# The pool of the small statistics tiles placed below the weights' buffers instead of above them

## The chip, the cores and the metric

The kernel runs on one core of a Trainium2 chip. The metric is the device time of one execution in microseconds (us); the time of a kernel is the median of its runs.

## The reference, cut to what matters

Two transformer blocks are applied one after the other to one sequence of 1024 tokens with 1024 features, all in float32. In outline:

```python
# block 1 (modulated by c; a context of 256 tokens takes part in its mixer)
x = x + g1 * token_mixer(modulate(rmsnorm(x), sh1, sc1), h_ctx)   # gated linear attention, spatial mix
x = x + g2 * swiglu(modulate(rmsnorm(x), sh2, sc2), w_ffn_in, w_ffn_out)
x = rmsnorm(x)
# block 2
proj = rmsnorm(x) @ w_in
x = x + (gate_a * rg_lru(...) + gate_b * banded_attention(...)) @ w_out
x = x + (silu(ff_gate) * ff_up) @ w_ffn_out                       # ff_gate, ff_up from rmsnorm(x) @ w_ffn_in
x = rmsnorm(x)
```

Nearly all of the work is in products of the activations (1024 tokens) with weights of 1024 by 1024 up to 1024 by 5632.

## The kernel before, in words

Activations lie feature-major, as tiles of 128 features by 512 tokens (float32, 2048 bytes per partition), one for each half q of the tokens. To reach float32's accuracy with float32r products, each operand is held as an exact sum of two parts, hi and lo, and each k step of a product is three matmuls: weight hi by activation hi, weight hi by activation lo, weight lo by activation hi. `gemm` (L163 to L165) does this for blocks of 128 by 128 weights, held stationary, and 512 tokens that move. `gemm_tok` (L175 to L177) turns the roles round: 128 tokens of the activations are stationary and 256 columns of weights move. `ffn_in` (L1051 to L1053) and `ffn_out` (L1264 to L1266) have their own three lines, with products by the scheme of Strassen and Winograd.

A block of weights goes through `unit` (L139 to L152): a DMA on SP's queue brings it into a tile of the pool raw, ScalarE copies it as the hi part into a tile wh (L150), and GpSimd, or VectorE, subtracts to get the lo part, a tile wl (L151). In the FFN the weights come into tiles of 512 columns, and `split` (L192, L193) writes half a wh and half a wl.

Order: the program is written out by hand. `proj` gives the products of one block of weights, `step` does them one after the other and after each of them `tick` takes one step of what runs beside them (norms, decays, the heads' attention), and in block 2 also half way through a product. Waits between engines are set by the framework from the tiles' uses.

Storage: SBUF pools are opened in `__init__` (L59 to L69) and lie one after the other in the order of their opening. Sizes are per partition.

- cst: constants, among them vt, ident and ones.
- raw: 2 tiles of 4096 bytes. wp: 4 tiles wh and 4 tiles wl of 4096 bytes. tmp: 4 tiles t512 of 2048 bytes.
- sm: the statistics tiles, 4 each of ms, rsy, rst, es and ast (32 bytes), 4 of et (64 bytes), and lc0 to lc4 once (64 bytes).
- hp: 32 tiles hl of 2048 bytes, for split activations.
- After hp come the pools of a phase: ada (2 tiles of 512 bytes), slots or lru (tiles of 4096 bytes), halves (44 tiles half of 2048 bytes), in block 2's mixers also kq, vhl, p, pt, bias and ot, all of sizes that are multiples of 512 bytes.

`ffn_out`, L1206 to L1215, does the last of its blocks of hidden features (4 k steps) in another way: all eight units of weights are loaded ahead and kept, and their parts lie in tiles hl of the pool hp, not in wh and wl:

```python
kept.append(self.unit(wo[m][:, cols], kt=n, into=[self.part(), self.part()]))
```

Its moving operands are tiles half. These products are at the end of each block's FFN, with 512 tokens in block 1 and for the first half of the tokens in block 2, and with 256 for the second half there.

Of the kernel before, what the change touches and what calls it, by code (L numbers as in the profile page):

```python
# [16 lines left out]
P = 128  # L17
T = 1024
# [31 lines left out]
def hs(q):  # L50
    """The columns of half q of the tokens."""
    return slice(q * HQ, q * HQ + HQ)


class Prog:
    """Activations lie feature-major, [features on partitions, tokens], in tiles of 128
    features by 512 tokens; operands of the large products as exact sums of two float32r parts."""

    def __init__(self, tc, ins, out, ctx):  # L59
        self.tc, self.nc, self.I, self.out = tc, tc.nc, ins, out  # L60
        self.cst = self.pool(ctx, "cst", 1)
        self.raw = self.pool(ctx, "raw", 2)
        self.wp = self.pool(ctx, "wp", 4)
        self.tmp = self.pool(ctx, "tmp", 4)
        self.sm = self.pool(ctx, "sm", 4)
        self.hp = self.pool(ctx, "hp", 32)
        self.dr = self.pool(ctx, "dr", 1, space=bass.MemoryType.DRAM)
        self.bg, self.lag, self.loads = deque(), deque(), 0

# [28 lines left out]
    def slot(self, *dims, dt=F32):  # L98
        """[P, 1024] of the phase's storage, or less of it in the shape dims."""
        return self.shaped(self.sp.tile([P, T], dt, name="slot"), dims)  # L100
# [7 lines left out]
    def half(self, dt=F32):  # L108
        """[P, 512] of the phase's storage."""
        return self.gp.tile([P, HQ], dt, name="half")  # L110
# [4 lines left out]
    def hnew(self, n=8):  # L115
        """A split activation, hi and lo, each n tiles of features by halves of tokens."""
# [22 lines left out]
    def unit(self, src, kt=8, width=P, eng=None, raw=None, into=None):  # L139
        """Load one block of weights (if it isn't in raw yet) and split it exactly into two float32r parts."""  # L140
# [13 lines left out]
    def wide(self, src, eng=None, raws=(None, None)):  # L154
        """Two blocks, 1024 x 256 together."""
        return [self.unit(src[i], kt=4, width=256, eng=eng if i else None, raw=raws[i]) for i in range(2)]

    def gemm(self, o, w, h, l, q, kt=8, s=slice(None), mid=None):
        """o[feature, token] = W^T X with both operands split; mid comes half way."""
# [9 lines left out]
    def gemm_tok(self, o, ws, h, l, t):  # L169
        """o[token, feature] = X W for the 128 tokens of block t."""  # L170
# [8 lines left out]
    def proj(self, src, fn, mid=None):  # L179
        """The products of one block of weights with both halves of the tokens."""  # L180
# [15 lines left out]
    def tick(self, n=1):  # L196
        """The next step of what runs beside the large products."""
# [14 lines left out]
    def store(self, dst, src):  # L212
        """A store that later loads need not wait behind."""
        self.lag.append((self.loads + 2, dst, src))
# [6 lines left out]
    def step(self, chunks, n=1):  # L221
        """One product after the other, with n steps of what runs beside them after each."""
# [5 lines left out]
    def square_into(self, acc, src, first, scale=1.0, eng=None):  # L228
        """acc += (scale * src)^2"""
# [6 lines left out]
    def squares(self, acc, src, eng):  # L236
        """The sum of the squares of tiles."""
# [4 lines left out]
    def token_sums(self, accs, ps, o):  # L242
        """ps[:, o + b] = sums over features for the tokens of block b."""
# [6 lines left out]
    def rsqrt(self, x):  # L250
        """1/sqrt of a small positive tile, by Newton's steps from the exponent's half."""
# [12 lines left out]
    def spread(self, r):  # L264
        """r holds a value for each token, tokens on partitions in blocks: the same on all
        partitions, tokens along the free axis."""
# [6 lines left out]
    def rstd(self, accs, n=D):  # L273
        """1/sqrt(mean of the squares + eps) in a bank, from sums of squares, in two steps."""
# [10 lines left out]
    def now(self, steps):  # L285
        """All steps at once."""
# [6 lines left out]
    def modulated(self, x, rs, A, B, hi, lo, eng=None):  # L293
        """hi + lo = x * A * rs + B"""
# [10 lines left out]
    def norm(self, q, acc, A, B=None):  # L305
        """Steps to the modulated norm of half q of self.x, in the form that ffn_in takes: with quarters Bij
        (i: half of the features, j: of the tokens), B11, B21, B22 and the sums T1..T4, all split."""
# [54 lines left out]
    def ada_first(self):  # L362
        """Shift and scale of the first norm, for the latents and the context, one half of the features after
        the other, by products; most of the scale by sums of weighted rows over k first. In steps."""
# [45 lines left out]
    def ada_one(self, m):  # L410
        """A block of gate 1, shift 2, scale 2, gate 2 of the latents; its sums over k and those of the
        block before over the partitions."""
# [19 lines left out]
    def ada_last(self):  # L432
# [5 lines left out]
        # the branches are summed twice as large  # L438
# [3 lines left out]
    def start(self):  # L442
# [5 lines left out]
        # resets of the scans at the chunks' first tokens  # L448
# [56 lines left out]
    def start_latents(self):  # L505
        """Steps to the norm of the latents."""
# [15 lines left out]
    def decays(self, st, n, zs, d):  # L522
        """Cumulated log decays (times GATE_TEMP) of direction d within each chunk, in steps.
        st: stacked low-rank inputs [96, n]; gives tiles that hold [P, NH, n] in order."""
# [29 lines left out]
    def low_rank(self, waf, st, h, l, n, q):  # L554
        """Inputs of the decays, stacked [hi; lo; hi]."""
# [23 lines left out]
    def latent_decays(self, stl, zs):  # L579
        """Decays of the latents, kept outside."""  # L580
# [36 lines left out]
    def context_states(self, st, zs):  # L617
        """Steps to the states that the context leaves, for both directions."""
        nc = self.nc
        self.Si = self.slots_of(2, NH, 256)  # L620
        for d in QS:
# [7 lines left out]
            # the half that is passed first decays through the other one too  # L629
# [17 lines left out]
    def ends(self, c, d):  # L647
        """Of chunked log decays: the chunks' totals, their exponentials, those of pairs."""
# [10 lines left out]
    def transposed(self, x):  # L659
        """Each block of 128 columns of x, transposed."""  # L660
# [9 lines left out]
    def gla_consts(self):  # L670
# [3 lines left out]
        for d in QS:  # L674
# [3 lines left out]
            # partition = key j, column = query i; forward j <= i  # L678
# [4 lines left out]
        # half of the norm's gain, for twice the silu  # L683
# [3 lines left out]
    def gla_proj(self, h, B):  # L687
        """Queries, keys and values of a head."""
# [20 lines left out]
    def gla_decayed(self, h, d, B):  # L709
        """Keys and queries with the decays of direction d."""  # L710
# [17 lines left out]
    def gla_dir(self, h, d, B, X):  # L728
        """Steps of one direction of a head."""
# [4 lines left out]
        for g in QS:  # L734
            ps = self.ax_bank()
            for i in range(4):
# [3 lines left out]
                # keys of the half passed first against queries of the other  # L740
# [51 lines left out]
    def gla_head(self, h, B):  # L792
        """Steps of a head: both directions, then the norm of the sum."""
# [27 lines left out]
    def gla_out(self, h, B, parts=None):  # L821
        """The gated output of a head, kept outside or split."""
# [17 lines left out]
    def gate_unit(self, nm, m, dst):  # L840
        """tanh of half a branch gate: its sigmoid is half of 1 + that."""
# [46 lines left out]
    def load_heads(self, parts):  # L888
        """Steps to the output of all heads, split; the last one's comes in its own way."""
# [21 lines left out]
    def spatial(self):  # L911
# [25 lines left out]
        # spatial weights, and the part of the mix that the shift of the norm and the bias give  # L937
# [55 lines left out]
    def residual(self, src, wo, h, l, scale, norm):  # L993
        """self.x = src + scale * (h + l) @ wo, one half of the tokens after the other, and the
        norm of each half"""
# [19 lines left out]
    def ffn_in(self, wi, hid):  # L1015
        """hid = silu(W_gate^T h) * (W_value^T h), by the products of Strassen's scheme in Winograd's form:
        the quarters of W^T are Aij (i: gate or value, j: half of the features)."""
# [55 lines left out]
        def ahead(f):  # L1073
            """The parts of A and their sums in the order of the products."""
# [23 lines left out]
        # the first products do without the second half of the tokens  # L1098
# [27 lines left out]
    def ffn_out(self, wo, hid, xs, scale, pieces, squares, norm, extra=lambda: iter(())):  # L1126
        """x += scale * FFN(h), by blocks of hidden features: plain products, or those of Strassen's scheme in
        Winograd's form (with quarters by pairs of tiles of x, halves of the block and halves of the tokens). The
        last block's sums come in pieces (half, columns), each followed by what norm gives for it."""
# [7 lines left out]
        def plain(f0, n, H):  # L1137
            """Steps to the operands of plain products."""
# [10 lines left out]
        def forms(f0, n, X):  # L1149
            """Steps to the operands of the scheme's products."""  # L1150
# [44 lines left out]
        def room(w):  # L1195
            """The next half of a buffer of weights, its two parts."""
# [5 lines left out]
        def supply():  # L1202
            """The weights of all products in order, each with its share of the buffers."""
# [73 lines left out]
        def residue():  # L1277
            """Steps that add what x was."""
# [92 lines left out]
    def between(self, q, accs, gg):  # L1371
        """Steps of the final norm of the first block, then the first norm of the second, for half q."""
# [9 lines left out]
        # 1 / sqrt(m1) / sqrt(m2 / m1 + eps) = 1 / sqrt(m2 + eps * m1)  # L1382
# [23 lines left out]
    def lru_consts(self):  # L1406
        """c8 = -8 softplus(-lambda) / 2, and halves of the gate biases."""
# [5 lines left out]
        # log1p(e) = 2 atanh(e / (2 + e))  # L1413
# [16 lines left out]
    def lru_front(self, j, F):  # L1430
        """The convolved input, also split."""
# [20 lines left out]
    def lru_gates(self, j, F):  # L1452
        """Products of the gates of both directions."""
# [16 lines left out]
    def lru_rest(self, j, F):  # L1470
        """Pieces of the gated linear recurrences; twice their values are halved here."""
# [12 lines left out]
        def rate(d):  # L1484
            # 1 - a^2 = tanh(-log a) (1 + a^2)
# [20 lines left out]
    def attention_consts(self):  # L1506
        """Distance and window terms of all heads, kept outside, in steps."""
# [6 lines left out]
        # 0 inside the window, -1e30 outside  # L1514
# [8 lines left out]
    def keys_values(self):  # L1523
        """Keys and values of all heads, kept outside."""
# [26 lines left out]
    def att_group(self, G):  # L1551
        """Keys of a group as [hi; hi] and [lo; lo], values as [hi | lo]."""
# [314 lines left out]
```

## Time and profile before

| | |
|---|---|
| median of 3 runs | 3458.62 us |
| lowest and highest run | 3456.98 and 3459.93 us |
| span of the profiled execution | 3453.9 us |
| TensorE busy | 3305.8 us, 15,868 matmuls |
| TensorE weight loads busy | 2683.4 us |
| VectorE, ScalarE, GpSimd busy | 2118.4, 1364.3, 1544.3 us |
| granted TensorE clock, mean | 0.985 |

The profile is of one execution; its span goes from the first to the last instruction, and the page gives no other time of that execution. The runs shown lie 3.1 to 6.0 us above the span, their median 4.7 us. PE is TensorE's matmul, PEld its weight load, DVE VectorE, ACT ScalarE, POOL GpSimd, SP the queue that issues most DMAs. Matmuls are pipelined: one of 512 columns is shown as some 0.4 us long while the next starts after 0.23 us, so that the pace is read from starts or from counts, not from durations. Times of windows count from the span's start. In a line such as `mm<-half,wh` the output stands first, then the moving operand, then the stationary one.

### The profile page before, as it was taken

The numbers are of one execution on the slowest core, as the hardware profiler recorded it, in microseconds if no ns is written. First come the engines' busy times: TensorE is split into PE (matmuls) and PEld (weight loads), VectorE is DVE, ScalarE is ACT, GpSimd is POOL, SyncE is SP. The second block draws the span as 40 slices with busy tenths as digits, with TensorE's granted clock in tenths as the row PEclk, the third lists the DMA queues.
The fourth block names the chain that finished last, engine by engine and source line by source line (L and its number), as shares of the span: only waits on it lengthen the run. The fifth ranks groups of instructions, "written<-read, shape, count | busy, mean of one in ns | idle before, by whom it ended". The sixth has DMA issues, their size and how long they took to land. (4 is left out here: it accounts for less than half of the span.)

```text
span 3453.9 us, 43238 instructions
## 1 busy us (share of the span) xinstructions
PE 3305.8 (96%) x15868; PEld 2683.4 (78%) x15868; DVE 2118.4 (61%) x3438; ACT 1364.3 (39%) x2396; POOL 1544.3 (45%) x991
## 2 busy tenths in 40 slices
PE   7999999999999999999999989999999999999997
PEld 4778888888888778888767867777777778887766
DVE  7554234333667385555698587777776585554786
ACT  4552222211122442232424486666665332232433
POOL 3222233222322675444656434444444775444764
PEclk9999999999999999999999999999999999999999
DMA  6121111244236522221352311111114432222342
GB/s 254 62 110 53 49 68 65 74 159 129 84 119 204 169 92 80 74 82 67 113 177 83 130 33 54 45 54 45 54 48 154 144 103 99 74 80 89 95 137 78
DMA packets 153012, 335.11 MB, mean 97 GB/s; under 512 B 20864, under 2 KB 29184, under 8 KB 152800
## 3 DMA queue, kind: packets, MB, share of 16 engines
q1 hardware_dynamic: 140640, 311.36, 26.8%
q10 hardware_dynamic: 12160, 20.98, 1.6%
q8 instruction: 126, 2.06, 0.2%
q14 instruction: 86, 0.70, 0.1%
HBM read 263.07 MB, written 69.21 MB: 96 GB/s over the span
## 5 line engine op out<-in xcount | busy, mean ns | idle before, releaser
L151 POOL TENSOR_TENSOR wl<-raw,wh 128x1024 fp32r<-128x1024 f32 (+1 forms) x188 | 426.7, 2273 | 751.2 <-ACT wh L150 629.9
L163 PE MATMUL mm<-hl,wh 128*128 128x512 f32 (+1 forms) x1584 | 643.3, 406 | 1.4 <-ACT t L1547 1.4
L165 PE MATMUL mm<-hl,wl 128*128 128x512 f32 (+1 forms) x1584 | 630.7, 398 | 1.6 <-POOL wl L151 1.6
L164 PE MATMUL mm<-hl,wh 128*128 128x512 f32 (+1 forms) x1584 | 631.7, 399 | 0.0
L193 POOL TENSOR_TENSOR wl<-half,wh 128x512 fp32r<-128x512 f32 x308 | 433.0, 1430 | 367.5 <-ACT wh L192 367.5
L150 ACT CAST wh<-raw 128x1024 fp32r<-128x1024 f32 (+3 forms) x189 | 177.4, 940 | 492.3 <-PE mm L164 232.4
L165 PEld LDWEIGHTS mm<-hl,wl 128*128 128x128 f32 (+1 forms) x1584 | 300.5, 190 | 74.6 <-POOL wl L151 2.4
L163 PEld LDWEIGHTS mm<-hl,wh 128*128 128x128 f32 (+1 forms) x1584 | 300.2, 190 | 66.6 <-ACT t L1547 1.8
L164 PEld LDWEIGHTS mm<-hl,wh 128*128 128x128 f32 (+1 forms) x1584 | 300.5, 190 | 64.9 <-issue 0.5
L192 ACT CAST wh<-half 128x512 fp32r<-128x512 f32 x308 | 178.6, 619 | 409.6 <-PE ax L1052 218.1
L1030 DVE TENSOR_TENSOR half<-half 128x512 f32<-128x512 f32 x176 | 202.1, 1188 | 3.0
L1606 POOL TENSOR_SCALAR p<-p,ast 128x384 f32<-128x384 f32 (+1 forms) x64 | 84.0, 1313 | 263.4 <-DVE ast L1604 162.5
L175 PE MATMUL mm<-wh,hl 128*128 128x256 f32 x576 | 163.5, 284 | 1.3 <-ACT wh L150 1.3
L177 PE MATMUL mm<-wl,hl 128*128 128x256 f32 x576 | 161.8, 281 | 1.9 <-POOL wl L151 1.9
L176 PE MATMUL mm<-wh,hl 128*128 128x256 f32 x576 | 162.2, 282 | 0.7 <-DVE hl L193 0.5
L1052 PE MATMUL mm<-hl,wh 128*128 128x512 f32 x360 | 142.8, 397 | 3.3 <-POOL hl L193 3.3
L1051 PE MATMUL mm<-hl,wh 128*128 128x512 f32 x360 | 142.6, 396 | 0.6 <-ACT hl L192 0.6
L1053 PE MATMUL mm<-hl,wl 128*128 128x512 f32 x360 | 142.4, 395 | 0.0
L1051 PE MATMUL ax<-hl,wh 128*128 128x512 f32 x344 | 136.5, 397 | 0.8 <-ACT hl L192 0.7
L1053 PE MATMUL ax<-hl,wl 128*128 128x512 f32 x344 | 136.2, 396 | 0.0
L1052 PE MATMUL ax<-hl,wh 128*128 128x512 f32 x344 | 136.0, 395 | 0.0
L193 POOL TENSOR_TENSOR wl<-raw,wh 128x384 fp32r<-128x384 f32 x96 | 113.8, 1204 | 37.1 <-ACT wh L192 37.1
(419 smaller groups left out, 7991.7 us busy)
## 6 DMA issues: line engine op xcount, KB each, us to landing
half<-in_w_fi SPq DMA_DIRECT2D x196, 256.0 KB, 4.7
hid<-t SPq DMA_DIRECT2D x78, 256.0 KB, 2.0
half<-hid SPq DMA_DIRECT2D x72, 256.0 KB, 4.5
raw<-in_w_ada SPq DMA_DIRECT2D x32, 512.0 KB, 3.7
raw<-in_w_o SPq DMA_DIRECT2D x32, 512.0 KB, 3.9
raw<-in_w_fo SPq DMA_DIRECT2D x32, 384.0 KB, 3.2
slot<-in_w_ada SPq DMA_DIRECT2D x16, 512.0 KB, 10.2
raw<-in_w_u SPq DMA_DIRECT2D x16, 512.0 KB, 3.6
```

Source lines behind the costliest of these rows:

```text
L150: nc.scalar.copy(hi, r)
L151: self.last_split = (eng or nc.gpsimd).tensor_tensor(lo, r, hi.bitcast(F32), op=ALU.subtract).ins
L163: mm(o, wh[:, k], h[k][q][:, s], start=k == 0, stop=False)
L164: mm(o, wh[:, k], l[k][q][:, s], start=False, stop=False)
L165: mm(o, wl[:, k], h[k][q][:, s], start=False, stop=k == kt - 1)
L175: mm(o, h[k][q][:, s], wh[:, k % 4], start=k == 0, stop=False)
L192: self.nc.scalar.copy(hi, x)
L193: (eng or self.nc.vector).tensor_tensor(lo, x, hi.bitcast(F32), op=ALU.subtract)
L1030: V.tensor_tensor(s, a, b, op=op)
L1051: mm(o, wh[:, k], h, start=k == 0, stop=False)
L1052: mm(o, wh[:, k], l, start=False, stop=False)
L1053: mm(o, wl[:, k], h, start=False, stop=k == 3)
```

## The change

In `__init__` the pool sm is opened right after cst, ahead of raw, wp and tmp, instead of after tmp. Nothing else in the code differs; comments and docstrings are gone.

```diff
         self.cst = self.pool(ctx, "cst", 1)
+        self.sm = self.pool(ctx, "sm", 4)
         self.raw = self.pool(ctx, "raw", 2)
         self.wp = self.pool(ctx, "wp", 4)
         self.tmp = self.pool(ctx, "tmp", 4)
-        self.sm = self.pool(ctx, "sm", 4)
         self.hp = self.pool(ctx, "hp", 32)
         self.dr = self.pool(ctx, "dr", 1, space=bass.MemoryType.DRAM)
```

## Rows read from the trace of the kernel before

**Rows 1.** The page's first part: busy us (share of the span) xinstructions.
```profile
PE 3305.8 (96%) x15868; PEld 2683.4 (78%) x15868; DVE 2118.4 (61%) x3438; ACT 1364.3 (39%) x2396; POOL 1544.3 (45%) x991
```

**Rows 2.** Windows: stretch, us, PE, PEld, DVE, ACT, POOL busy (x), PEclk, DMA share, GB/s.
```profile
110.00:660.00 550.00, 538.86 (x3022) 458.18 (x3021) 213.37 (x300) 175.16 (x251) 141.88 (x59) 0.98 0.19 67
660.00:820.00 160.00, 156.82 (x703) 126.65 (x702) 64.43 (x131) 30.67 (x44) 42.97 (x22) 1.00 0.45 147
...
920.00:1200.00 280.00, 278.26 (x1275) 226.94 (x1276) 173.06 (x295) 79.25 (x114) 108.70 (x58) 0.99 0.47 158
1200.00:1650.00 450.00, 443.10 (x1890) 353.01 (x1890) 275.90 (x331) 144.65 (x253) 243.33 (x171) 1.00 0.23 80
1650.00:1860.00 210.00, 193.79 (x790) 150.40 (x789) 179.87 (x227) 79.90 (x156) 132.03 (x100) 0.97 0.40 132
1860.00:2660.00 800.00, 753.31 (x3659) 613.09 (x3658) 587.96 (x1172) 514.75 (x964) 340.50 (x192) 0.98 0.19 64
2660.00:3170.00 510.00, 504.10 (x2158) 402.08 (x2157) 297.87 (x363) 161.79 (x276) 290.39 (x197) 1.00 0.29 100
3170.00:3390.00 220.00, 206.24 (x845) 157.44 (x844) 155.35 (x197) 80.60 (x161) 145.47 (x115) 0.98 0.38 120
```

**Rows 3.** Windows, same columns: inside ffn_in, inside the kept block of block 1.
```profile
1300.00:1600.00 300.00, 300.00 (x1287) 241.74 (x1286) 169.75 (x200) 86.70 (x153) 148.59 (x108) 1.00 0.23 81
1862.00:1886.00 24.00, 24.00 (x107) 19.87 (x106) 15.35 (x23) 14.90 (x24) 7.08 (x5) 1.00 0.25 78
```

**Rows 4.** Timeline of PE in ffn_in: start us, us, engine, line, op, tiles.
```profile
1399.83 0.39 PE L1052 MATMUL ax<-half,wh 128*128 128x512 f32 x1
1400.06 0.40 PE L1053 MATMUL ax<-half,wl 128*128 128x512 f32 x1
...
1402.40 0.40 PE L1051 MATMUL mm<-half,wh 128*128 128x512 f32 x1
```

**Rows 5.** Timeline of PE at the start of the kept block, same columns.
```profile
1859.00 0.39 PE L163 MATMUL mm<-half,hl 128*128 128x512 f32 x1
...
1860.39 0.39 PE L163 MATMUL mm<-half,hl 128*128 128x512 f32 x1
...
1862.88 0.39 PE L165 MATMUL ax<-half,hl 128*128 128x512 f32 x1
```

**Rows 6.** Windows, matmuls that read wl alone: stretch, us, PE busy (x), PEclk, DMA.
```profile
110.00:660.00 550.00, 242.24 (x688) 0.98 0.19 67
660.00:820.00 160.00, 86.53 (x222) 1.00 0.45 147
...
920.00:1200.00 280.00, 145.56 (x367) 0.99 0.47 158
1200.00:1650.00 450.00, 247.08 (x626) 1.00 0.23 80
1650.00:1860.00 210.00, 106.27 (x262) 0.97 0.40 132
1860.00:2660.00 800.00, 320.13 (x820) 0.98 0.19 64
2660.00:3170.00 510.00, 280.84 (x711) 1.00 0.29 100
3170.00:3390.00 220.00, 111.09 (x278) 0.98 0.38 120
```

**Rows 7.** Windows, columns of rows 2: inside gemm_tok of the spatial mix.
```profile
845.00:875.00 30.00, 30.00 (x257) 30.00 (x257) 10.29 (x45) 6.34 (x13) 4.84 (x3) 1.00 0.30 106
```

**Rows 8.** Timeline of PE, kept block of block 2 with 256 columns.
```profile
3413.04 0.28 PE L165 MATMUL ax<-half,hl 128*128 128x256 f32 x1
...
3415.20 0.28 PE L165 MATMUL mm<-half,hl 128*128 128x256 f32 x1
```

**Rows 9.** The page's DMA issues: tiles, queue, count, KB each, us to landing.
```profile
half<-in_w_fi SPq DMA_DIRECT2D x196, 256.0 KB, 4.7
...
raw<-in_w_o SPq DMA_DIRECT2D x32, 512.0 KB, 3.9
```

## The prediction

> **What bounds the kernel now.** I read the page's busy times first, then stretches of the run one by one, then the starts of single products. TensorE is busy 3305.8 of the 3453.9 us [rows 1], but matmuls overlap, so this alone does not say at what pace they run. By stretches [rows 2], the PE column covers 98 to 100% of 660 to 1650 us and of 2660 to 3170 us at a granted clock of 0.99 to 1.00, while VectorE stays under 62% and GpSimd under 58% there. In these stretches only a shorter distance from one matmul to the next can shorten the run. In 1650 to 1860 and 3170 to 3390 PE has 92 and 94%, and 1860 to 2660 has 94% with VectorE at 73%: there PE also waits, and a faster PE gives part of its gain back as a longer wait. 110 to 660 has 98%, but its products are cut up by the small ones of the attention heads.
>
> So the distance of the products is the question. From 1300 to 1600 us PE does nothing but 512-column products of ffn_in, whose weights lie in wh and wl: 1286 weight loads in 300 us are 233.3 ns each [rows 3]. From 1862 to 1886 us it does nothing but products of the same shape (128 rows by 128 columns by 512, L163 to L165, four k steps) whose weights lie in hl, since ffn_out's last block keeps its weights in the activations' pool: 106 loads in 24 us, 226.4 ns each. The starts say the same: 11 steps in 2.57 us are 233.6 ns [rows 4], 11 steps in 2.49 us are 226.4 ns [rows 5]. Clock (1.00), moving operand (half) and reading engine are the same; VectorE, ScalarE and GpSimd work beside both. What differs is where the weights lie.
>
> **What the change moves.** sm holds per partition four each of ms, rsy, rst, es and ast (32 bytes) and et (64 bytes), and lc0 to lc4 once (64 bytes): 4 x 224 + 320 = 1216 bytes, which is 2 x 512 + 192. Raw (2 x 4096), wp (8 x 4096) and tmp (4 x 2048) are 49,152 bytes, 96 x 512. Before, hp follows sm, so hl and all pools above it (whose tiles are multiples of 512 bytes) lie 192 bytes off wh and wl modulo 512. After, sm sits below, raw, wp and tmp move up by 1216, and hp stays where it was: weights and activations have one phase, as hl and half have now in the block at 1862 us. The sm tiles move down by 96 x 512 and keep their phase. The phases agree even modulo 2048, as in that block, since 49,152 is 24 x 2048. No instruction, wait or DMA is added, removed or reordered on any queue, SP's and POOL's included.
>
> **The price of one product.** I take the two settled steps as the prices: 233.3 - 226.6 = 6.7 ns saved by each 512-column product with weights in wh or wl. 226.4 is not there at once: after the switch to the kept weights the first six steps take 1.39 us, 231.7 ns each, and only then comes 226.4 [rows 5]. A run that is broken every dozen products by other work would thus spend half of it unsettled, and I count nothing for these steps.
>
> Here a rule of the Trainium skill speaks against the change. Its page "TensorE: Matmul & The Clock Gate", section "Step-by-step: what each phase is for", says that PE has two independent read ports into SBUF, so that loading the next weights takes nothing from the running matmul. By it the place of the weights is without effect and the sum would be 0; the two settled steps, 233.3 and 226.4, leave a difference which it does not account for.
>
> **The sum.** Each k step has two products with wh and one with wl, so the products are three times the count of wl [rows 6], less the 640 k steps of gemm_tok where wl is the moving operand: by the code 256 in 110 to 660 (values of four heads), some ten at the end of 660 to 820 and 64 in 1860 to 2660, the rest outside the table. For each stretch: products, the share that runs settled (from the length of unbroken runs in the code: whole units of 24 and more, against attention with 12 or less), and the share of the gain that stays on the path.
> - 1200 to 1650 (ffn_in): 1878 x 0.95 x 1.0 = 1784, 12.0 us.
> - 2660 to 3170 (w_out and ffn_in of block 2): 2133 x 0.95 x 0.95 = 1925, 12.9 us.
> - 920 to 1200: 1101 x 0.80 x 0.9 = 793, 5.3 us. 660 to 820: 639 x 0.85 x 0.9 = 489, 3.3 us.
> - 110 to 660 (heads of block 1): 1296 x 0.65 x 0.4 = 337, 2.3 us.
> - 1860 to 2660 (mixers): 2268 x 0.35 x 0.6 = 476, 3.2 us. The scores, softmax and turned weights of a block wait for each other on VectorE and ScalarE, so much of the time between two waits of PE is theirs.
> - 1650 to 1860 and 3170 to 3390 (ffn_out): 1620 x 0.75 x 0.3 = 365, 2.4 us. The next limit there is the split weights and VectorE's sums, which do not get faster.
> Together 41.4 us. The path shares of 1 and 0.9 are read from PE's coverage; 0.3 to 0.6 are choices between 0 and 1, and the range carries both ends.
>
> Against it, gemm_tok: its 256-column products have hl as weights and wh, wl as the moving operand, and they too come into one phase. They now take 30 us for 257 [rows 7], 117 ns; the kept block's 256-column products, already of one phase, take 18 steps in 2.16 us, 120.0 ns [rows 8]. 1920 x 3 ns are up to 5.8 us of loss; the two rows differ in operand roles, so the other end is 0. I take 4.4 us.
>
> Other engines: the splits, loads and sums on raw, wh, wl and t512 now start 192 bytes further on. Transfers into half already start there and take 4.7 us, those into raw 3.9 us [rows 9]; the sizes differ, so this bounds a dearer landing at 0.8 us. It is covered by the two raw buffers and up to four of wh and wl that are filled ahead of PE. I cost it at nothing; without that cover (the first unit of a stage) some ten loads would cost 8 us. A gain for these engines is as possible and also hidden.
>
> Sum: 41.4 - 4.4 = 37.0 us, about 1.1%. The span of 3453.9 would become 3416.9. The median of the runs shown, 3458.62, lies 4.7 above that span; the same distance gives 3421.6, and I say 3421.6.
>
> **The rivals.**
> (a) No effect, 3459 to 3463: the kept weights are faster for another reason (they were written long before, or lie far from address 0), and 0 to 4.4 us of gemm_tok remain. For: by the code only 288 products have 512 columns and kept weights. Against: VectorE, ScalarE and GpSimd are at work in both windows of [rows 3], so it is not their traffic that makes the difference. Also here: the pools are not placed in the order in which they are opened, so that no phase changes.
> (b) Slower, 3486: one phase is what costs. The 256-column rows show it, 120 against 117 ns; if products on freshly written weights in wp behave like those, 10,965 x 3 ns x 0.65 on the path + 5.8 = 27 us. Place: every product with wh or wl. It decides once the mean step rises by 0.2 ns (7 us is the bound of no change, less gemm_tok's 5). Against: the same shape with 512 columns is shorter at one phase.
> (c) Only long streams gain, 3438: runs cut by other work never settle or return all to their waits, and 12.0 + 12.9 - 4.4 = 20.5 us are left. For: the six slow steps after each break. Nearly the same time, 3441, comes out if nothing settles and every product saves 1.6 ns as these six do.
>
> **How the numbers follow.** Forecast 0.73, (c) 0.13, (a) 0.09, (b) 0.05. The range reaches from all path shares at 1 and no loss in gemm_tok, 8090 x 6.7 = 54.2 us, 3404, to (c), 3440; (a) and (b) stay outside. 0.2%, some 7 us, is about what a measurement of this kernel can tell from no change: faster 0.86, same 0.09, slower 0.05.
>
> **What would show it.** Right: 300 us inside ffn_in hold 1323 loads instead of 1286, the steps there are 0.23 and 0.22 us in turn, gemm_tok's go to 0.12; PE's coverage in 1200 to 1650 and 2660 to 3170 stays, these stretches shorten by about 12 us each, and PE's waits grow in ffn_out. Wrong: settled steps of 233 ns in ffn_in with kept ones still at 226 (a), or above 234 (b); or 226 in ffn_in but no shortening behind it, so that a wait I do not see took it.

## The result and the profile after

The changed kernel takes 3423.12 us (median of 4 runs, 3417.93 to 3424.86) against 3457.95 for the kernel before (median of 4), a ratio of 0.9897, 95% interval 0.9883 to 0.9911. The prediction said 3421.6 and 3404 to 3440. The profiled execution's span goes from 3453.9 to 3422.2 us.

The page's first part after the change, against [rows 1]: as many matmuls, 45.7 us less of PE, 11.9 more of its weight loads, the other engines within 9 us of what they had.

```profile
PE 3260.1 (95%) x15868; PEld 2695.3 (79%) x15868; DVE 2126.6 (62%) x3438; ACT 1363.1 (40%) x2396; POOL 1539.2 (45%) x991
```

The pace, against [rows 3]: windows (stretch, us, PE, PEld, DVE, ACT, POOL busy with counts, PEclk, DMA share, GB/s) inside ffn_in and inside the kept block of block 1.

```profile
1290.00:1590.00 300.00, 300.00 (x1325) 248.51 (x1324) 178.59 (x209) 88.23 (x157) 151.84 (x111) 1.00 0.24 80
1839.00:1863.00 24.00, 24.00 (x107) 19.88 (x106) 17.81 (x25) 13.08 (x22) 5.90 (x6) 1.00 0.29 88
```

In ffn_in 300 us now hold 1324 weight loads, 226.6 ns each, where 1286 stood; the prediction asked for 1323. The kept block, whose weights did not move against its activations, has 106 as before. One load lasts as long as it did, 187.7 ns against 188.0 (PEld's time by its count); it is the distance from product to product that shrank. The timeline of PE in ffn_in, against [rows 4], shows the new step:

```profile
1389.71 0.39 PE L1051 MATMUL ax<-half,wh 128*128 128x512 f32 x1
...
1392.20 0.39 PE L1053 MATMUL ax<-half,wl 128*128 128x512 f32 x1
```

Eleven steps in 2.49 us, 226.4 ns, which is the kept block's settled step [rows 5].

Where the 31.7 us of span came from is read by cutting the new run at the same matmuls at which the old one was cut in [rows 2] (each border is the new start of the product that stood at the old border; 820 to 920 is added). Same columns as above:

```profile
110.00:656.70 546.70, 533.85 (x3023) 460.01 (x3022) 212.94 (x300) 175.19 (x251) 141.91 (x59) 0.98 0.20 67
656.70:815.90 159.20, 153.89 (x702) 127.67 (x702) 65.41 (x133) 30.59 (x44) 42.91 (x22) 0.99 0.46 149
815.90:917.60 101.70, 101.17 (x794) 98.62 (x793) 39.81 (x169) 19.24 (x41) 26.22 (x16) 0.98 0.27 91
917.60:1190.20 272.60, 270.37 (x1275) 226.09 (x1276) 175.38 (x295) 78.49 (x114) 107.12 (x58) 1.00 0.49 162
1190.20:1629.30 439.10, 430.94 (x1890) 352.51 (x1889) 277.39 (x332) 144.24 (x253) 243.41 (x172) 1.00 0.24 82
1629.30:1837.10 207.80, 189.81 (x790) 149.54 (x789) 178.82 (x224) 79.59 (x155) 129.35 (x100) 0.97 0.41 133
1837.10:2639.00 801.90, 749.74 (x3659) 616.36 (x3658) 592.63 (x1174) 515.31 (x965) 340.91 (x193) 0.97 0.20 64
2639.00:3138.20 499.20, 491.97 (x2158) 402.89 (x2157) 299.31 (x363) 161.52 (x276) 289.79 (x197) 1.00 0.30 103
3138.20:3357.70 219.50, 204.08 (x845) 160.22 (x844) 155.16 (x197) 81.07 (x162) 145.60 (x115) 0.97 0.38 120
```

The second number of each row is the length. 1200 to 1650 (ffn_in), 2660 to 3170 (w_out, then ffn_in of block 2) and 920 to 1200 carry the gain: 10.9, 10.8 and 7.4 us. 1860 to 2660, with its 2268 products, became 1.9 us longer; 660 to 820 gained 0.8 us.

Two places show where gain went missing. In 656.7 to 815.9 PE waits twice for the first weights of gemm_tok (waits of PE: tile, line, releaser, us in total, times, longest), after and then before:

```profile
PE mm L175 <- ACT wh L150: 3.4, 1, 3.4
PE mm L177 <- POOL wl L151: 1.9, 1, 1.9
```
```profile
PE mm L177 <- POOL wl L151: 1.9, 1, 1.9
PE mm L175 <- ACT wh L150: 1.3, 1, 1.3
```

wh came 2.1 us later against PE than before. And the clock fell after it, in both kernels, but longer in the kernel after: windows right behind, the columns as above, after and then before.

```profile
813.00:817.00 4.00, 3.84 (x18) 3.84 (x19) 1.65 (x5) 0.00 (x0) 0.11 (x1) 0.50 0.94 284
817.00:821.00 4.00, 4.00 (x27) 4.00 (x27) 1.53 (x7) 0.66 (x2) 0.00 (x0) 0.73 0.67 234
```
```profile
820.00:824.00 4.00, 4.00 (x25) 4.00 (x25) 2.75 (x8) 0.03 (x1) 0.00 (x0) 0.67 0.73 230
824.00:828.00 4.00, 4.00 (x36) 4.00 (x35) 0.87 (x4) 1.41 (x3) 0.00 (x0) 1.00 0.42 143
```

PE had just waited 5.3 us, against 3.2 before. The next eight microseconds hold 45 products after and 61 before: at a granted clock of 0.50, the lower of the two levels (1.2 GHz), a product takes twice as long (18 in four microseconds, 36 at 1.00).

In 1837.1 to 2639 PE idles 52.2 us (801.90 less 749.74), 5.5 more than in [rows 2]. Waits of PE there, after and then before:

```profile
...
PE sc L1595 <- DVE pt L193: 11.8, 13, 1.9
PE po L1630 <- DVE slot L1635: 8.9, 8, 1.2
PE po L1630 <- ACT pt L192: 4.6, 8, 0.7
...
PE ax L270 <- DVE rsy L261: 1.3, 1, 1.3
```
```profile
...
PE sc L1595 <- DVE pt L193: 11.0, 12, 1.7
PE po L1630 <- DVE slot L1635: 8.3, 8, 1.2
PE po L1630 <- ACT pt L192: 2.0, 6, 0.3
```

The turned weights of the softmax (pt) take VectorE 0.52 us and ScalarE 0.45 us a tile in both traces, and the norm's rsqrt (rsy) takes VectorE 0.16 us an operation in both. What grew is PE's idle time ahead of them: these rows by 2.6, 0.8 and 0.6 us, and the wait for rsy, 1.3 us, is new: 5.3 together.

The stretch's net loss lies in its first 70 us, not in the attention where most of these waits are. Two products behind 1860, the last one ahead of rsy and one 37 us later, in the timeline of PE before and then after:

```profile
1893.29 0.39 PE L165 MATMUL ax<-half,hl 128*128 128x512 f32 x1
...
1930.66 0.40 PE L165 MATMUL mm<-hl,wl 128*128 128x512 f32 x1
```
```profile
1870.35 0.39 PE L165 MATMUL ax<-half,hl 128*128 128x512 f32 x1
...
1910.64 0.39 PE L165 MATMUL mm<-hl,wl 128*128 128x512 f32 x1
```

Ahead of rsy the kernel after leads by 22.9 us, at the second product by 20.0. About half of the 2.9 us is the wait for rsy; the other half is lost where the clock stands at 0.50, from 1898 us on, behind 16 products of one column each. From there to 2660 the lead grows again by 1.0 us.

### The profile page after: what moved, and what is told of

It reads as the page before. It is cut to its first block, busy times and chain, and to the rows that moved or that the text cites. A ratio compares the mean times of both kernels' runs of the same rounds, so it can differ in the third digit from the quotient of the medians.

```text
span 3422.2 us, 43238 instructions
## 1 busy us (share of the span) xinstructions
PE 3260.1 (95%) x15868; PEld 2695.3 (79%) x15868; DVE 2126.6 (62%) x3438; ACT 1363.1 (40%) x2396; POOL 1539.2 (45%) x991
## 5 line engine op out<-in xcount | busy, mean ns | idle before, releaser
L163 PE MATMUL mm<-hl,wh 128*128 128x512 f32 (+1 forms) x1584 | 636.8, 402 | 1.6 <-ACT t L1547 1.4
L164 PE MATMUL mm<-hl,wh 128*128 128x512 f32 (+1 forms) x1584 | 624.2, 394 | 0.0
```

The source lines that it names most:

```text
L163: mm(o, wh[:, k], h[k][q][:, s], start=k == 0, stop=False)
L164: mm(o, wh[:, k], l[k][q][:, s], start=False, stop=False)
```

## The experiments

All kernels leave the arithmetic as it is. "Distance" is the address of the activations (hp and all pools above it) less that of the weights (wp), modulo 512 bytes; it is 192 before and 0 after. Each ratio is to the kernel before, run beside it.

**What counts: the distance or a place.** Two kernels take the change apart. The first keeps the new order and restores the distance:

```diff
         self.tmp = self.pool(ctx, "tmp", 4)
+        self.pool(ctx, "pad", 1).tile([P, 48], F32, name="pad")
         self.hp = self.pool(ctx, "hp", 32)
```

> The changed kernel (sm below the weights), with 192 unused bytes between tmp and hp: wh and wl stay at phase 192 as in the changed kernel, the activations go to 384, so the distance of the two is 192 again, as before the change. Theory (only the distance modulo 512 counts): 512-column steps in ffn_in go back to 233.3 ns, 1286 loads in 300 us there, gemm_tok's steps back to 117 to 118 ns, time that of the kernel before within 0.2% (3451 to 3465 us). Rival 1 (the weights' own place counts, phase 192 is good and 0 bad): 226.6 ns and about 3423 us stay. Rival 2 (it is good that the statistics tiles no longer lie between tmp and hp): 226.6 ns and about 3423 us stay.

Measured: 3456.98 us against 3458.6, ratio 0.9998 [0.9989, 1.0008]. Windows, columns as above:

```profile
1300.00:1600.00 300.00, 300.00 (x1287) 241.71 (x1286) 171.03 (x202) 86.80 (x153) 146.72 (x107) 1.00 0.24 81
1862.00:1886.00 24.00, 24.00 (x107) 19.89 (x106) 16.38 (x24) 14.37 (x24) 7.17 (x6) 1.00 0.28 87
```

All of the gain is gone with 192 bytes that nobody reads, and the loads of ffn_in are the 1286 of before. The kept block has its 106 also here, so the activations' new place did no harm. The second kernel keeps the old order and removes the distance, by moving 192 bytes out of sm:

```diff
-        e, z, z2, s, m = (self.sm.tile([P, 16], F32, name=f"lc{i}", bufs=1) for i in range(5))
+        e, z, z2, s, m = ((cst if i < 3 else self.sm).tile([P, 16], F32, name=f"lc{i}", bufs=1) for i in range(5))
```

> The kernel before, its pools in their old order, with lc0, lc1 and lc2 (192 bytes) in cst instead of sm: sm is 1024 bytes, raw, wp and tmp move up by 192, hp stays. The distance of weights and activations is 0 modulo 512 with sm still between them. Theory: 226.6 ns in ffn_in, 120 ns in gemm_tok, the time of the changed kernel, 3423 us within 0.2%. Rival 1 (the weights' own phase 192): the same, so this run does not tell it apart. Rival 2 (place of sm): 233.3 ns and 3458 us.

Measured: 3422.5 us, ratio 0.9896 [0.988, 0.9913].

```profile
1300.00:1600.00 300.00, 300.00 (x1325) 248.43 (x1324) 176.33 (x205) 88.71 (x158) 151.17 (x110) 1.00 0.24 81
```

The order of the pools is without effect; the distance is the whole change. Raw and tmp moved against the activations together with wp in all these kernels; that it is not their traffic is read from the kept block, which has 226.4 ns with raw and tmp 192 bytes off the activations (the kernel before) and at distance 0 alike. A third kernel moves both sides: a pad of 288 bytes ahead of raw in the kernel after.

> The kernel after with 288 unused bytes ahead of raw: raw, wh, wl, t512 and all pools of the activations start 288 bytes further on, at 480 modulo 512, and keep distance 0. Theory 1 (the distance alone counts): 226.8 ns, gemm_tok's 119.9 ns, about 3423 us. Rival (the own phase of each operand counts too, or DMAs and vector engines are dearer at another phase): steps other than 226.8 ns, or the same steps and a time off 3423 us by over 7 us.

Measured: 3422.83 us against 3458.48, ratio 0.9906 [0.9892, 0.9921], and 1325 loads:

```profile
1300.00:1600.00 300.00, 300.00 (x1325) 248.47 (x1325) 178.11 (x207) 88.60 (x157) 151.94 (x112) 1.00 0.24 81
```

Neither side's own phase counts, at the two places tried.

**How near the phases have to be.** The same pad ahead of hp, in other sizes. A quarter and a half of 512:

> The changed kernel with 64 unused bytes between tmp and hp: distance 64. Theory: the steps depend on the distance and only 0 is known to be short; some value above 227 ns, at most 236, and 3425 to 3460 us. If multiples of 64 bytes were enough (a rival of finer grain), 226.6 ns and 3423 us stay. Rival 1 and 2: 226.6 ns and 3423 us stay too.

> The changed kernel with 256 unused bytes between tmp and hp: distance 256, half of the period of 512. Theory: above 227 ns, at most 236; 3425 to 3460 us. If the period is 256 and not 512, 226.6 ns and 3423 us stay. Rival 1 and 2: 226.6 ns and 3423 us stay.

At 64 the time is 3432.99 us, ratio 0.992 [0.9903, 0.9936], between the two as the theory allowed; at 256 it is 3422.12, ratio 0.9892 [0.9877, 0.9907]. The window 1300 to 1600 of the kernel with 64 and of that with 256:

```profile
1300.00:1600.00 300.00, 300.00 (x1313) 246.15 (x1312) 178.05 (x206) 87.52 (x156) 150.87 (x109) 1.00 0.24 81
```
```profile
1300.00:1600.00 300.00, 300.00 (x1325) 248.43 (x1324) 178.07 (x207) 88.62 (x157) 151.41 (x111) 1.00 0.24 81
```

At 256 the theory missed: with half of 512 between them the operands are as good as with none. So the period is at most 256 bytes, or 256 is a second good place. Four more kernels ask for the period and for the shape in between; 320 is the kernel before with 128 bytes ahead of hp.

> The kernel before with 128 unused bytes ahead of hp: the activations lie 320 bytes off the weights modulo 512, which is 64 modulo 256. Theory 1 (only the distance modulo 256 counts): all as in gap64, settled 512-column steps of wh and wl 229.6 ns, gemm_tok's 115.7 ns, about 3433 us. Rival (a period of 512, with a second good place at 256): 320 is a place of its own, nothing forces it to 229.6; its mirror image 192 would give 233.3 ns and 3458 us.

Measured: 3428.24 us, ratio 0.9918 [0.9902, 0.9935], an interval that holds the 0.992 of 64, and the loads of 64, 1312:

```profile
1300.00:1600.00 300.00, 300.00 (x1313) 246.13 (x1312) 178.01 (x206) 88.60 (x157) 150.75 (x109) 1.00 0.24 81
```

With 0 and 256 alike and 64 and 320 alike the period of 256 stands for two pairs.

> The kernel after with 128 unused bytes ahead of hp: distance 128, half of a period of 256. Theory 1 (a cost that grows with the distance from 0 up to 192: 226.8 at 0, 229.6 at 64, 233.3 at 192): a step between 229.6 and 233.3, about 231.5 ns, and about 3445 us. Rival (a cost symmetric about half the period, so that 64 and 192 are not mirror images by chance of something else): the worst place, above 233.3 ns and above 3458 us.

> The kernel after with 32 unused bytes ahead of hp. Theory 1 (a cost that grows evenly with the distance): 512-column steps about 228.2 ns, gemm_tok's about 117.8 ns (between 119.9 at 0 and 115.7 at 64), about 3427 us. Rival (the distance counts in grains of 64 bytes): steps as at 0, 226.8 ns, with gemm_tok's between 115.7 and 119.9; 3419 to 3423 us.

Measured: 128 gives 3455.96 us, ratio 0.9992 [0.9983, 1.0002]; 32 gives 3458.98 us, ratio 1.0004 [0.9994, 1.0013]. First the window of 128, then that of 32:

```profile
1300.00:1600.00 300.00, 300.00 (x1288) 241.34 (x1287) 170.03 (x200) 85.43 (x151) 148.46 (x108) 1.00 0.24 80
```
```profile
1300.00:1600.00 300.00, 300.00 (x1287) 241.02 (x1286) 169.87 (x200) 85.69 (x151) 148.24 (x108) 1.00 0.24 80
```

For 128 both missed: the step is that of before (233.1 ns by the count, 300 us over 1287), at the very edge of the theory's bracket and 11 us over its time, and it is not dearer either. For 32 both expectations missed: 32 bytes cost as much as 192. A cost that grows with the distance is out.

> The kernel after with 96 unused bytes ahead of hp. Theory (the distance modulo 256 counts, in grains of 64 bytes, and what is off the grain by 32 is as dear as the kernel before): settled 512-column steps of ffn_in at 233.4 ns, about 3455 us. Rival (one line between 229.6 at 64 and 232.8 at 128): 231.2 ns, 3442 us.

> The kernel after with 160 unused bytes ahead of hp. Theory (as for 96): 233.4 ns, about 3455 us. Rival (a line between 232.8 at 128 and 233.3 at 192 gives nearly the same here, 233.0 ns): this place alone does not tell the two apart, it fills the table.

> The kernel after with 224 unused bytes ahead of hp. Theory (off the grain of 64 by 32): 233.4 ns, about 3455 us. Rival (a cost by the distance to the nearest multiple of 256, 32 here, on the other side than in gap32, where 233.4 was measured): 233.4 ns too if both sides are alike; between 226.8 and 233.3 ns, 3423 to 3455 us, if the two sides differ.

One profile each: spans of 3459.6, 3458.2 and 3453.9 us against 3453.9 before. Windows of 96, of 160 and of 224:

```profile
1300.00:1600.00 300.00, 300.00 (x1288) 241.31 (x1287) 172.37 (x203) 85.76 (x152) 147.10 (x107) 1.00 0.24 81
```
```profile
1300.00:1600.00 300.00, 300.00 (x1282) 241.14 (x1282) 171.33 (x203) 85.88 (x152) 146.04 (x106) 1.00 0.24 81
```
```profile
1300.00:1600.00 300.00, 300.00 (x1287) 241.54 (x1286) 170.40 (x201) 86.74 (x153) 147.53 (x108) 1.00 0.24 81
```

So of the eight places at 32 bytes from each other, 0 gives 226.5 ns, 64 gives 228.7, and all others lie between 233.1 and 234.0 (300 us by the counts; 160 alone has the 234.0). That 96 would equal before was right to one load in 300 us; that it lies off a grain of 64 is no reason for it, since 128 and 192 lie on the grain and are as dear. Why 64 alone keeps some two thirds of the gain stays open.

**A wait that took the gain.** In the kernel after, the second block's load for gemm_tok waits until GpSimd has split the first. The first two blocks go to VectorE instead:

```diff
-            ws = self.wide(I["w_v"][cg])
+            ws = [self.unit(I["w_v"][cg][i], kt=4, width=256, eng=None if cg else V) for i in range(2)]
```

> The kernel after with the first two blocks of weights of gemm_tok (cg 0 in spatial) split by VectorE, not GpSimd. Theory (the gain of 660 to 820 is given back because the second block's load waits for the first one's wl on GpSimd, 2.40 us, and its own wl takes GpSimd as long; VectorE takes 1.23 us for such a tile and is idle there): the load starts 1.2 us earlier, the second wl is there 2.4 us earlier, PE's products after it stand 6.0 us ahead of the kernel before at 830 us where the kernel after has 3.6; about 3420.7 us, which the times cannot tell from 3423. Rival (the queue of DMAs sets when the second block lands, and the split does not): 1.2 us or nothing, 3.6 to 4.8 us ahead. Further rival: the gain of 2.4 us at 830 is lost again in the next wait and is not there at 1030.

Measured: 3422.67 us, ratio 0.9901 [0.9885, 0.9918], which the times can't tell from the kernel after, as was said. In the trace the waits before gemm_tok's second block are 3.2 us instead of 5.3, and the clock stays at 1.00:

```profile
PE mm L175 <- ACT wh L150: 2.4, 1, 2.4
PE mm L177 <- DVE wl L151: 0.8, 1, 0.8
```
```profile
809.00:813.00 4.00, 3.24 (x27) 3.08 (x26) 2.46 (x5) 0.91 (x1) 0.00 (x0) 1.00 0.68 178
813.00:817.00 4.00, 4.00 (x36) 4.00 (x35) 1.45 (x5) 0.66 (x2) 0.00 (x0) 1.00 0.79 282
```

PE's products at 830 us stand 9.6 us ahead of the kernel before, where 6.0 was expected and the kernel after has 3.7 (starts of the same products in both traces, of which 1 us was there before 660 already). The theory had the wait and not the clock: with 36 products in four microseconds against 18, the clock returns about as much as the wait. That it stays up after 3.2 us of waiting is one execution: in the kernel before the same 3.2 us were followed by 0.67. Of these 5.9 us, 2.3 were lost again by 1030, as the further rival has it in part: there PE stands 9.2 us ahead against 5.6, and at the end 35.1 against 31.8. The span of tok_dve, 3418.8 us, is the shortest that was profiled; other executions of the kernel after went down to 3416.1.

How long PE waits for wh here also differs between kernels of one step. The seven profiles with the old step have 1.2 to 3.3 us, the four of distance 0 or 256 with GpSimd's split 3.4 to 4.0. The 3.3 is in the kernel with 128 (whose pad moves its lines down by one):

```profile
PE mm L176 <- ACT wh L151: 3.3, 1, 3.3
```

So PE's earlier arrival lengthens the wait, but of the 2.1 us between the two profiles above some part is the difference of single executions.

## Why the prediction was right

**The step.** It took 233.3 and 226.6 ns from rows of the same run, and the changed kernel has 226.6 by the count. The reading that the place of the weights against the activations makes the difference, and not how the kept weights were written or what else was at work, is shown by the pads and by lc_moved, which change nothing else. With it rival (a) falls, and (b), which wanted a dearer step at one phase. (By the list of stretches (b)'s 10,965 products are 10,935, which changes nothing in its 27 us; and in ffn_in not every moving operand is a half, some are tiles hl of the same phase.) The rule weighed there (the Trainium skill, "TensorE: Matmul & The Clock Gate", "Step-by-step: what each phase is for") has it that loading the next weights takes nothing from the running matmul. What the prediction drew from it, that the place of the operands is without effect, does not hold in these rows: the same pair takes 226.5, 228.7 or 233 ns and more by the distance of its operands alone. Why the distance counts, and whether it is the two reads that hinder each other, no run shows.

**The sum**, predicted gain of each stretch and what the lengths above give. Each length is of one execution. Cut at the same products, the six profiles with pads that keep the old step differ from the kernel before by up to 2.5 us in a stretch; the four other kernels of distance 0 or 256 (lc_moved, both480, the one with 256, tok_dve) are given as "the four".
- 1200 to 1650: 12.0, came 10.9 (the four: 10.9 to 11.3). 2660 to 3170: 12.9, came 10.8 (10.3 to 12.1). PE's idle time grew by 1.3 us in each (450.00 less 443.10 against 439.10 less 430.94, likewise in the other), which the path shares of 1.0 and 0.95 had not left room for. All 10.8 us of the second came behind 2770, in ffn_in (10.8 in the four too); the 110 us of w_out ahead of it gained nothing, with 3.1 us of waits there instead of 0.3 (the four: -0.5 to 1.3).
- 920 to 1200: 5.3, came 7.4 (6.0 to 7.7): the share there was too low. 110 to 660: 2.3, came 3.3 (1.2 to 4.2), which the spread does not tell apart.
- 660 to 820: 3.3, came 0.8. Up to 812 the gain was there, 3.8 us, and 3.7 to 3.8 in the four. The wait for gemm_tok's first weights, which DMA and splits set, took the rest with the clock behind it, and part of that is chance: four of the six with pads and the old step lost 1.3 to 2.5 us in this stretch as well. The prediction had read coverage (156.82 of 160 us) and not what stands at the stretch's end.
- 1860 to 2660: 3.2, came -1.9 (the four: -2.2 to 2.3). This is the term that failed, by its path share of 0.6. The products did get shorter (PE's busy time fell by 3.6 us), but idle time grew by 5.5. Rival (c), that what is cut by other work returns its gain to its waits, holds at most in this one stretch and not in the others. The loss at its start is in all five: each waits 1.2 to 1.3 us for rsy, which no profile with the old step does. Four of the five also have the clock at 0.50 there and lose 3.0 us in all; the one with 256 keeps it at 1.00 and loses 1.4.
- ffn_out: 2.4, came 2.7 (2.2 and 0.5; the four together 0.7 to 1.8). Its idle time grew by 1.8 and 1.7 us, as was forecast.
- gemm_tok: a loss of 4.4 by 1920 products. The 768 of 820 to 920 made that stretch 1.7 us longer, 2.2 ns each; by that 1920 lose 4.2. The 3 ns per product were too much and the path share too little.

These lengths sum to 32.3 us, the remaining stretches lose 0.6, and the span shows 31.7 where 37.0 was forecast. By the medians it is 34.8 us. That the predicted time is off by 1.5 us only is in part luck: the span of the profiled execution before lay 4.7 us below the median, that of the one after 0.9 us. As an execution's time is some 1.7 us above its span in all runs on record, the first of the two was fast by 3.0 us and the second slow by 0.8.

**The other engines** were costed at nothing; both480, which shifts raw, wh, wl and t512 once more, has the time of the kernel after to 0.3 us.

**What it did not count is the clock.** A longer wait can be followed by the lower level for longer, as in the windows at 813 to 821. The mean granted clock, after and before (core, span, clock):

```profile
core 0: 3422.2 us, clock 0.981
```
```profile
core 0: 3453.9 us, clock 0.985
```

(1 - 0.981) x 3422.2 is 65.0 us of lost full speed, (1 - 0.985) x 3453.9 is 51.8. At most 13 us went that way; how many of them lie in idle time, where they cost nothing, was not separated. The difference is not that of two executions alone: the kernel after has 0.980 to 0.983 in its four executions, the kernel before 0.982 to 0.987 in all of its own. Only the first wait was tried, in tok_dve, and the mean clock of its four executions, 0.979 to 0.983, is no higher; the waits of 1860 to 2660 were read and not removed.

## What to carry to other kernels

Where a tuned kernel is bound by matmuls in a row, compare the step of the same shape with operands from different pools, and read the two operands' addresses modulo 256: 32 unused bytes between two pools cost 3% of every 512-column product here, and a pool's place in the list is enough to get them back. Put small and odd tiles below or above all large pools, not between them. Then look for what PE now reaches too early: where 2.1 us of waiting were taken away, the clock behind it gave back about as much again, in one execution. And read a stretch in several kernels of the same step before a term of one or two microseconds is called right or wrong.

## What the runs showed that was not expected

- The period is 256 bytes, as far as two pairs of places show, not the 512 by which the prediction reckons: 0, 256 and both sides at 480 give 1324 or 1325 loads in 300 us, 64 and 320 both 1312, and 32, 96, 128, 160, 192 and 224 from 1282 to 1287.
- The 256-column products of gemm_tok, whose moving operand is the weights, do not follow the same distances: 257 in 30 us at a distance of 192 [rows 7], 253 at 0. At 64 they keep the 257:

```profile
845.00:875.00 30.00, 30.00 (x257) 30.00 (x257) 9.07 (x39) 6.34 (x13) 7.20 (x3) 1.00 0.28 93
```
```profile
845.00:875.00 30.00, 30.00 (x253) 30.00 (x252) 8.86 (x38) 6.33 (x13) 7.11 (x3) 1.00 0.25 89
```

(the kernel with 64, then the kernel after). It isn't simply the other way round, either: the kernel with 160, the dearest place for 512 columns, has as few as 252, and the kernel with 224, dear there too, has the most, 260:

```profile
845.00:875.00 30.00, 30.00 (x252) 30.00 (x251) 9.74 (x42) 6.25 (x13) 4.78 (x2) 1.00 0.31 106
```
```profile
845.00:875.00 30.00, 30.00 (x260) 30.00 (x259) 13.08 (x56) 5.29 (x12) 4.81 (x2) 1.00 0.29 97
```

A version with distance 0 for the 512-column products and 64 for gemm_tok was not tried: both read their weights from one pool. Nor is it shown why the two shapes differ.
